# Two transformer blocks on one core: new durations in the instruction planner, and the low weight parts made on VectorE

## The chip, the cores and the metric

The kernel runs on one core of a Trainium2 chip. The metric is device time in microseconds (us) of one launch. Engine names are those of the profile: PE (TensorE matmul), PEld (its weight load), DVE (VectorE), ACT (ScalarE), POOL (GpSimd) and SP (SyncE, which here only issues DMAs).

## The reference

512 tokens of width 1024 go through two blocks, in fp32.

```python
# first block
h = rmsnorm(x); z = h @ w_in                      # 1024 x 5120
y_a = pool_mixer(z_pool) @ w_branch_a             # running means over 2, 4, 8, 16 tokens
y_b = spatial_gating(gelu(z_uv)) @ w_branch_b
x = x + (g_a * y_a + g_b * y_b) @ w_out
x = x + conv_ffn(rmsnorm(x))                      # w_up, 3-tap convolution in time, gelu(a) * b, w_down
x = x + sigmoid(rmsnorm(x) @ w_ple_gate) * (p @ w_ple)
x = rmsnorm(x)
# second block, two layers
for i in range(2):
    x = x + 0.5 * swiglu(rmsnorm(x))              # 1024 x 2816, twice, and back
    x = x + (sliding_window_attention, latent_attention)[i](rmsnorm(x))
    x = x + 0.5 * swiglu(rmsnorm(x))
```

## The kernel before

**Precision.** Each fp32 operand of a large product is split into a high part in the matmul type fp32r and a low part, the rest. `mm` (L710) then makes one product from three matmuls: high by high, high by low, low by high. So 128 rows of depth by 512 tokens are three matmuls of 128x512. For activations, `split` makes the high part on ACT and the low part on DVE. For weights, `Weights._make` (L599) loads a chunk of 128x1024 (`wr`, three buffers), casts it on ACT (`wh`, four buffers) and subtracts on POOL (`wl`, four buffers); it runs three chunks ahead of the chunk in use. Only the first chunk is subtracted on DVE, in four quarters.

**Stages, in order.** Mixer; convolutional feed-forward; the p branch; final norm and first swiglu; sliding-window attention; two swiglus; latent attention; last swiglu. A feed-forward stage (`up_down`, L908) makes 12 pairs of projections (each projection 24 matmuls of 128x512), then half of the way down, then 10 pairs, then the other half. Activations lie transposed, features on partitions and the 512 tokens in the free dimension, as eight tiles x0 to x7.

**Norms.** A stage begins with `operands` and `rstd_tok`: for each x tile a split (ACT high, DVE low, written to `op`), a square on ACT (`f`) and a DVE sum `f<-f`. Four small matmuls with the column `mcol` turn the sum into a mean for each token (`pt<-mcol,f`). PE fills the time until then with the first projections of the stage.

**The convolutional stage.** Each pair takes on DVE two reads of PSUM (`f<-ps,f`), four `SCALAR_TENSOR_TENSOR` (`f<-f,vec`), one product and one split. In the background, one chunk a pair, runs the bias of the later sliding-window attention (`plan_bias`, L1046): six DVE operations of 128x512 (`e<-poshi`, `e<-e,poslo`, `g<-e,poslo`), 24 small matmuls on PE (`pt<-rbp,g`) and two DVE additions of 128x256 (`e<-pt,con`).

**Order.** Nothing is issued where the code stands. The program is first recorded (class `Order`, L368), then `arrange` runs a list schedule: five engines with clocks of their own, a duration for each instruction (`_cost`), a latency of 150 ns from any instruction to one that depends on it (`LAT`), a transfer model, and the buffers of every pool. At each step an engine takes the ready instruction that stands first in the program and finds its buffers free. The order that results is what each engine's queue executes in sequence, on the chip with real durations: an instruction whose input is late holds up all behind it on its engine. All instructions are emitted by L586, so the profile names that line throughout; tiles tell them apart.

Of the kernel before, what the change touches and what calls it, by code (L numbers as in the profile page):

```python
# [10 lines left out]
F32 = mybir.dt.float32  # L11
# [29 lines left out]

# 1 / (2 pi) in parts of 11 bits
INV_2PI = 159154943091895335768883763372514362034459645740456448747667344
# [5 lines left out]

# ---------------------------------------------------------------- host layout  # L50

# [198 lines left out]

# ------------------------------------------------------------- issue order
#
# The program is first traced with tiles and views that stand for the real ones,
# then every engine's instructions are put in the order in which a list schedule
# over rough costs would start them, and emitted so.

# [98 lines left out]
class Instr:  # L355
    __slots__ = ("eng", "name", "args", "kw", "deps", "tiles", "cost", "new", "table", "n", "ready", "bytes", "key",
                 "rows")

# [9 lines left out]
class Order:  # L368
    LAT = 150.0
    TABLES = {AF.Gelu: "g", AF.Silu: "s", AF.Sin: "s", AF.Sigmoid: "d", AF.Exp: "e"}  # L370
# [12 lines left out]
    def _cost(self, o):  # L383
        kw, a = o.kw, o.args
        if o.name == "dma_start":
            return 60.0
        if o.eng == "tensor":
            if o.name == "transpose":
                return 107.0
            n = math.prod(kw["rhs"].shape[1:])  # L390
            dt = kw["rhs"].dtype
            if dt == F32R:
                return max(n / 2.4 + 0.5, 56.0)
            return 4 * (n / 2.4 + 2.5) if dt == F32 else max(n / 2.4 + 2.5, 27.0)
        out = kw["out"] if "out" in kw else a[0]
        src = kw.get("in_", kw.get("in0", out))
        n = max(self._size(out), self._size(src))
        psum = any(isinstance(v, View) and v.base.pool.pool_psum for v in list(kw.values()) + list(a))
        if o.eng == "scalar":
            extra = sum(isinstance(kw.get(k), View) for k in ("scale", "bias", "accum_out"))  # L400
            near = isinstance(src, View) and src.base.pool.pool_psum
            return n / 1.2 + (51 if near else 95) + 93 * extra
        if o.eng == "vector":
            if o.name == "memset":
                return 20.0
            if o.name == "reciprocal":
                return 6.3 * n + 70
            fast = o.name in ("tensor_copy", "tensor_scalar") and not psum
            extra = sum(isinstance(kw.get(k), View) for k in ("scalar", "scalar1"))
            return n / (1.92 if fast else 0.96) + 70 + 59 * extra  # L410
        if o.name == "memset":
            return 50.0
        return (3.4 if o.name == "tensor_copy" else 2.24) * n + 80

    def add(self, eng, name, args, kw):
# [28 lines left out]
        o.table = self.TABLES.get(kw.get("func")) if eng == "scalar" else None  # L444
        o.cost = self._cost(o)
        o.rows = kw["rhs"].shape[0] / P if "rhs" in kw else 1.0
        o.bytes = 0
# [5 lines left out]

    def arrange(self):
        import heapq
        count, uses = {}, {}
# [15 lines left out]
        table, dma = None, 0.0  # L472
        warm, busy, window = False, 0.0, 0.0
        done = []
# [7 lines left out]
        def fits(o):  # L482
            need = {}
            if any(id(b) not in placed and b not in o.new for b in o.tiles):
                return False
            for b in o.new:
                need[b.slot] = need.get(b.slot, 0) + 1
            for k, c in need.items():
                if free[k] < c:
                    return False  # L490
                if free[k] < c + SPARE.get(k[1], 99):
                    f, i = fifo[k], head[k]
                    while c:
                        if id(f[i]) not in placed:
                            if f[i] not in o.new:
                                return False
                            c -= 1
                        i += 1
            return True

        while len(out) < len(self.ops):
# [8 lines left out]
            for e in engines:  # L510
# [41 lines left out]
                if o.table is not None and o.table != table:  # L552
                    table = o.table
                    c += 1283.0
                clock[e] = now + c
                end = now + c
                if o.bytes:
# [4 lines left out]
                for x in after[o.n]:  # L562
                    x.ready = max(x.ready, end + (0.0 if x.eng == o.eng == "tensor" else self.LAT))
                    count[x.n] -= 1
# [7 lines left out]
            if not nxt:  # L572
                if progress:
                    continue
                stuck = [(e, self.ops[n].name, n, [b.name for b in self.ops[n].new]) for e in engines
                         for _, n in sorted(able[e])[:2]]
                raise RuntimeError(f"no order found: {stuck}")
            now = min(nxt)
        return out

# [8 lines left out]

# ---------------------------------------------------------------- on the chip  # L590

class Weights:
# [7 lines left out]
    def _make(self):  # L600
# [8 lines left out]
        for o in range(0, n, step):  # L609
            c = slice(o, o + step)  # L610
            nc.sync.dma_start(out=raw[:, c], in_=src[:, c])
            nc.scalar.copy(out=h[:, c], in_=raw[:, c])
            (nc.vector if first else nc.gpsimd).tensor_tensor(out=lo[:, c], in0=raw[:, c], in1=h[:, c].bitcast(F32),
                                                              op=ALU.subtract)
# [13 lines left out]
class Core:  # L628
# [79 lines left out]

    # products of operands in two exact parts
    def mm(self, ps, w, x, start, stop):  # L710
# [82 lines left out]

    # ------------------------------------------------------------ first block
    def mixer(self):
# [209 lines left out]

    # ----------------------------------------------------------- second block
    def final_and_ffn(self):
# [30 lines left out]

    # relative-position bias and mask of the sliding window, one table entry at
    # a time by thresholds of the distance  # L1040
    def plan_bias(self):
# [79 lines left out]
    def attn_a(self):  # L1121
# [12 lines left out]

        # heads of 64 columns brought to length one, in place
        def norms(fs, tag):
# [32 lines left out]
        norms(kf, "k")  # L1169
        # keys of the two groups side by side, zero where the groups do not meet  # L1170
        kb = [self.opp.tile([P, 2, S], F32R, name="op", tag="op") for _ in range(2)]
# [114 lines left out]

    # sine and cosine of position times frequency, by exact reduction in turns
    def plan_rope(self):
# [61 lines left out]
    def attn_b(self):  # L1350
# [6 lines left out]
        nc.vector.tensor_copy(out=idb, in_=self.c("id", P))  # L1357
        # latents and the shared key part, tokens on partitions, two token tiles at a time
        wl = []
# [48 lines left out]

        # one over the length of four heads of 96 columns in four token tiles
        def lengths(ss, tag):  # L1410
# [77 lines left out]

        # keys of tile st against queries st..3, three banks
        dst = [(0, 0), (1, 0), (2, 0), (1, 3 * P)]  # L1490
# [153 lines left out]
```

## Time and profile before

| | |
|---|---|
| three timed runs | 2784.25, 2785.83, 2788.27 us |
| span of the profiled execution, first to last instruction | 2782.1 us |
| PE busy in it | 2679.4 us (96%) |
| DVE, ACT, POOL busy | 1376.1 (49%), 954.7 (34%), 1225.4 us (44%) |
| subtraction of the low weight parts on POOL | 1107.6 us in 467 instructions |
| granted TensorE clock, mean | 0.983 |

The page gives no time for the profiled execution but its span. The median of the runs is 3.7 us above it: what lies before the first and behind the last instruction. PE's busy time is a union of modelled spans: in a stretch in which PE never waits it reads 100%.

### The profile page before, as it was taken

How to read it: one execution, taken by the hardware profiler on the slowest of the kernel's cores; microseconds unless marked ns; L12 is line 12 of the kernel's file. 1: busy time of each engine (PE TensorE's matmuls, PEld its weight loads, DVE VectorE, ACT ScalarE, POOL GpSimd, SP SyncE). 2: the span in 40 equal slices, each digit the busy share in tenths (PEclk: the TensorE clock that was granted, in tenths of full speed). 3: DMA queues.
4: the chain of work that ended last, by engine and by line, in shares of the span. 5: the costliest groups of instructions: out<-in, count | busy, mean ns of one | idle time of the engine just before them, and what ended most of it. 6: DMA issues, size and time to landing. Idle time of an engine off the chain costs nothing. (4 is left out here: it accounts for less than half of the span.)

```text
span 2782.1 us, 32524 instructions
## 1 busy us (share of the span) xinstructions
PE 2679.4 (96%) x12768; PEld 2187.3 (79%) x12768; DVE 1376.1 (49%) x2193; ACT 954.7 (34%) x1486; POOL 1225.4 (44%) x664
## 2 busy tenths in 40 slices
PE   7999998999799899999999999999999899999999
PEld 5788886888677788889778888888888766688887
DVE  5506369949937861335743313343133676533141
ACT  3324333323334222334633223323223475432221
POOL 4543443353334344444534444444444443344443
PEclk9999999999899999999999999999999999999999
DMA  4232223333323333333222233322333201233322
GB/s 148 95 99 89 93 92 102 93 114 106 91 70 97 99 99 98 99 99 105 78 84 93 97 99 99 97 86 97 98 99 96 58 12 31 72 99 99 98 92 83
DMA packets 102617, 254.31 MB, mean 91 GB/s; under 512 B 37360, under 2 KB 39024, under 8 KB 102464
## 3 DMA queue, kind: packets, MB, share of 16 engines
q1 hardware_dynamic: 101840, 250.26, 28.4%
q8 instruction: 101, 1.65, 0.2%
q0 software_dynamic: 624, 1.97, 0.2%
q14 instruction: 52, 0.43, 0.1%
HBM read 242.76 MB, written 9.44 MB: 91 GB/s over the span
## 5 line engine op out<-in xcount | busy, mean ns | idle before, releaser
L586 PE MATMUL ps<-op,wh 128*128 128x512 f32 x6624 | 2069.9, 393 | 35.9 <-ACT op L586 24.4
L586 POOL TENSOR_TENSOR wl<-wr,wh 128x1024 fp32r<-128x1024 f32 (+3 forms) x467 | 1107.6, 2374 | 1393.3 <-ACT wh L586 1380.0
L586 PEld LDWEIGHTS ps<-op,wh 128*128 128x128 f32 x6624 | 1250.5, 189 | 304.7 <-ACT op L586 27.0
L586 PE MATMUL ps<-op,wl 128*128 128x512 f32 x3312 | 1299.7, 392 | 0.0
L586 ACT CAST wh<-wr 128x1024 fp32r<-128x1024 f32 (+3 forms) x471 | 468.1, 994 | 1236.7 <-PE ps L586 760.4
L586 PEld LDWEIGHTS ps<-op,wl 128*128 128x128 f32 x3312 | 627.4, 189 | 132.2 <-issue 1.0
L586 DVE TENSOR_TENSOR f<-ps,f 128x512 f32<-128x512 f32 x260 | 178.8, 688 | 532.9 <-PE ps L586 510.9
L586 DVE TENSOR_TENSOR op<-f,op 128x512 fp32r<-128x512 f32 x136 | 226.2, 1665 | 68.8 <-ACT op L586 68.0
L586 DVE TENSOR_TENSOR f<-f 128x512 f32<-128x512 f32 x213 | 203.1, 954 | 46.0 <-POOL f L586 19.8
L586 DVE SCALAR_TENSOR_TENSOR x<-ps,x 128x512 f32<-128x512 f32 x64 | 44.2, 691 | 339.0 <-PE ps L586 339.0
L586 ACT CAST op<-f 128x512 fp32r<-128x512 f32 x136 | 84.2, 621 | 211.1 <-DVE f L586 211.1
L586 PE MATMUL ps<-wh,op 128*128 128x256 f32 (+3 forms) x608 | 149.9, 333 | 4.8 <-ACT f L586 2.5
L586 PEld LDWEIGHTS ps<-wh,op 128*128 128x128 f32 x608 | 106.0, 194 | 15.6 <-ACT f L586 3.1
L586 ACT ACTIVATE f<-f 128x512 f32<-128x512 f32 x142 | 89.0, 627 | 77.8 <-DVE f L586 77.1
L586 DVE SCALAR_TENSOR_TENSOR f<-f,vec 128x512 f32<-128x512 f32 x88 | 104.5, 1188 | 8.9 <-ACT f L586 8.6
L586 DVE SCALAR_TENSOR_TENSOR op<-x,vec,op 128x512 fp32r<-128x512 f32 x64 | 84.4, 1324 | 48.1 <-ACT op L586 48.1
L586 PE MATMUL ps<-wl,op 128*128 128x256 f32 (+3 forms) x304 | 100.4, 330 | 0.0
L586 DVE TENSOR_TENSOR x<-ps,x 128x512 f32<-128x512 f32 x56 | 38.4, 688 | 98.6 <-PE ps L586 98.6
L586 ACT ACTIVATE op<-x,vec 128x512 fp32r<-128x512 f32 x64 | 45.8, 721 | 73.1 <-DVE x L586 72.8
L586 PE MATMUL pt<-con,opf 128*128 128x128 f32 (+1 forms) x348 | 54.5, 280 | 8.2 <-DVE opf L586 3.5
L586 PEld LDWEIGHTS ps<-wl,op 128*128 128x128 f32 x304 | 59.0, 194 | 3.5 <-issue 0.3
L586 DVE TENSOR_TENSOR g<-e,poslo 128x512 bf16<-128x512 f32 x56 | 61.4, 1098 | 0.1
(181 smaller groups left out, 1366.1 us busy)
## 6 DMA issues: line engine op xcount, KB each, us to landing
wr<-in_w SPq DMA_DIRECT2D x411, 512.0 KB, 3.3
wr<-in_w SPq DMA_DIRECT2D x40, 256.0 KB, 2.7
bias<-e SPq DMA_DIRECT2D x28, 256.0 KB, 2.7
opf<-bias SPq DMA_DIRECT2D x16, 448.0 KB, 6.0
x<-in_xT SPq DMA_DIRECT2D x8, 256.0 KB, 6.7
out_y<-x SPq DMA_DIRECT2D x8, 256.0 KB, 2.0
wr<-in_w SPq DMA_DIRECT2D x4, 416.0 KB, 3.1
wr<-in_w SPq DMA_DIRECT2D x12, 128.0 KB, 2.1
```

Source lines behind the costliest of these rows:

```text
L586: getattr(getattr(self.nc, o.eng), o.name)(*[real(a) for a in o.args], **{k: real(v) for k, v in o.kw.items()})
```

## The change

Five things. (1) `Weights._make` subtracts on DVE for every chunk, no longer on POOL. (2) The durations in `_cost` are other numbers: a 128x512 matmul in fp32r costs the planner 227.0 ns instead of 213.8, an fp32 matmul and a bf16 one a little less, POOL's operations 2.0 or 2.35 ns an element instead of 3.4 or 2.24. (3) The latency is a number for each engine. (4) The planner has a `port`: POOL's compute instructions, and those DVE instructions that `_port` names, start one after another in its model. (5) `arrange` tries again with more spare buffers where a plan sticks, in place of an error.

```diff
-    LAT = 150.0
+    LAT = {"tensor": 203.0, "vector": 111.0, "scalar": 128.0, "gpsimd": 90.0, "sync": 34.0}
...
             if dt == F32R:
-                return max(n / 2.4 + 0.5, 56.0)
+                return max(n / 2.4 + 13.7, 56.0)
...
+    def _port(self, o):
+        if o.eng == "gpsimd":
+            return o.name != "dma_start"
+        if o.eng != "vector" or o.name == "memset":
+            return False
+        vs = [v for v in list(o.kw.values()) + list(o.args) if isinstance(v, View) and self._size(v) > 1]
+        near = [v for v in vs if not v.base.pool.pool_psum]
+        if o.name in ("tensor_copy", "tensor_scalar"):
+            return len(near) == len(vs)
+        return o.name in ("tensor_tensor", "scalar_tensor_tensor", "tensor_tensor_reduce") and len(near) > 2
...
-                clock[e] = now + c
-                end = now + c
+                begin = now
+                if o.port:
+                    begin = max(now, port)
+                    port = begin + c
+                clock[e] = begin + c
+                end = begin + c
...
             nc.scalar.copy(out=h[:, c], in_=raw[:, c])
-            (nc.vector if first else nc.gpsimd).tensor_tensor(out=lo[:, c], in0=raw[:, c], in1=h[:, c].bitcast(F32),
+            nc.vector.tensor_tensor(out=lo[:, c], in0=raw[:, c], in1=h[:, c].bitcast(F32),
                                                               op=ALU.subtract)
```

What the new plan does to the queues is seen at three places. The first is DVE at the end of the latent attention, where each of the last projections is added to an x tile (`x4<-ps`), split (`op<-x4,vec`), and its square added to the sum (`f<-f`). Before, from x4 to x6:

```order
L586 TENSOR_TENSOR x4_125<-ps_18271,x4_125 128x512
L586 SCALAR_TENSOR_TENSOR op_18308<-x4_125,vec_84,op_18308 128x512
L586 TENSOR_TENSOR f_18212<-f_18212,f_18313 128x512
L586 TENSOR_TENSOR x5_127<-ps_18298,x5_127 128x512
L586 SCALAR_TENSOR_TENSOR op_18335<-x5_127,vec_84,op_18335 128x512
L586 TENSOR_TENSOR x6_129<-ps_18321,x6_129 128x512
```

And in the changed kernel, over the same tiles:

```order
L617 TENSOR_TENSOR x4_121<-ps_18272,x4_121 128x512
L617 TENSOR_TENSOR wl_18304<-wr_18233,wh_18296 128x1024
L617 SCALAR_TENSOR_TENSOR op_18307<-x4_121,vec_84,op_18307 128x512
L617 TENSOR_TENSOR f_18211<-f_18211,f_18311 128x512
L617 TENSOR_TENSOR x5_123<-ps_18298,x5_123 128x512
L617 TENSOR_TENSOR wl_18331<-wr_18259,wh_18321 128x1024
L617 SCALAR_TENSOR_TENSOR op_18334<-x5_123,vec_84,op_18334 128x512
L617 TENSOR_TENSOR x6_125<-ps_18324,x6_125 128x512
```

One weight subtraction now stands between each addition to an x tile and its split; the rest keeps its order. The second place is DVE in the second half of the convolutional stage, with the bias in the background. Before, somewhat under one pair:

```order
L586 TENSOR_TENSOR f_4734<-ps_4936,f_2873 128x512
L586 TENSOR_TENSOR e_4981<-e_4981,poslo_2999 128x512
L586 TENSOR_TENSOR e_5004<-poshi_2979 128x512
L586 SCALAR_TENSOR_TENSOR f_5000<-f_4734,vec_84,f_5000 128x512
L586 TENSOR_TENSOR g_4974<-e_4981,poslo_2999 128x512
L586 SCALAR_TENSOR_TENSOR f_5000<-f_4734,vec_84,f_5000 128x512
```

In the changed kernel, from a read of PSUM on:

```order
L617 TENSOR_TENSOR f_4776<-ps_4861,f_2868 128x512
L617 TENSOR_TENSOR e_4831<-pt_4906,con_129 128x8x32
L617 TENSOR_TENSOR e_4839<-pt_4906,con_129 128x8x32
L617 TENSOR_TENSOR wl_4944<-wr_4763,wh_4903 128x1024
L617 SCALAR_TENSOR_TENSOR f_4937<-f_4776,vec_84,f_4937 128x512
L617 TENSOR_TENSOR e_4958<-poshi_2975 128x512
L617 SCALAR_TENSOR_TENSOR f_4937<-f_4776,vec_84,f_4937 128x512
```

A subtraction stands between each read of PSUM and the first operation on it, two for a pair, and all of the bias work is still there. The third place is PE at the very start, around the four matmuls that make the first mean (`pt<-mcol`). Before, in the middle of the second projection:

```order
L586 MATMUL ps_224<-op_168,wl_222 128x512
L586 MATMUL ps_224<-op_172,wh_212 128x512
L586 MATMUL pt_253<-mcol_86,f_143 128x1 x4
L586 MATMUL ps_224<-op_172,wh_212 128x512
L586 MATMUL ps_224<-op_172,wl_222 128x512
```

In the changed kernel, in the middle of the third:

```order
L617 MATMUL ps_225<-op_162,wh_217 128x512 x2
L617 MATMUL ps_225<-op_162,wl_234 128x512
L617 MATMUL pt_284<-mcol_86,f_137 128x1 x4
L617 MATMUL ps_225<-op_166,wh_217 128x512 x2
L617 MATMUL ps_225<-op_166,wl_234 128x512
```

The mean is asked for 21 matmuls later. In the later norms PE's order is the same to within a few matmuls.

## Rows read from the trace of the kernel before

**Rows 1.** Cores: span and mean granted TensorE clock.
```profile
core 0: 2782.1 us, clock 0.983
```
**Rows 2.** PE's waits, whole span: total us, times, longest.
```profile
PE pt L586 <- DVE f L586: 30.4, 10, 6.7
PE ps L586 <- ACT op L586: 24.8, 6, 14.6
PE pt L586 <- DVE g L586: 11.8, 6, 4.5
```
**Rows 3.** Stretches: length, busy us (x instructions) per engine, granted clock, DMA share, GB/s.
```profile
430.00:475.00 45.00, 33.99 (x214) 26.70 (x214) 43.52 (x57) 13.08 (x17) 18.88 (x7) 0.96 0.29 87
...
741.00:766.00 25.00, 8.21 (x23) 5.53 (x22) 21.52 (x27) 8.59 (x12) 7.48 (x3) 0.59 0.26 83
...
1459.00:1816.00 357.00, 357.00 (x1575) 295.28 (x1574) 117.70 (x118) 106.11 (x128) 165.90 (x66) 1.00 0.30 96
...
2180.00:2243.00 63.00, 51.69 (x254) 42.58 (x253) 50.53 (x176) 35.27 (x81) 25.77 (x45) 0.92 0.16 45
...
2411.00:2425.00 14.00, 7.55 (x26) 6.06 (x25) 9.15 (x21) 2.72 (x4) 4.82 (x3) 0.63 0.26 77
```
**Rows 4.** Groups by form, whole span, DVE and POOL: busy us, mean ns, idle before.
```profile
L586 DVE TENSOR_TENSOR op<-f,op 128x512 fp32r<-128x512 f32 x136 | 226.2, 1665 | 68.8 <-ACT op L586 68.0
L586 DVE TENSOR_TENSOR f<-f 128x512 f32<-128x512 f32 x213 | 203.1, 954 | 46.0 <-POOL f L586 19.8 <-ACT f L586 16.1
L586 DVE TENSOR_TENSOR f<-ps,f 128x512 f32<-128x512 f32 x260 | 178.8, 688 | 532.9 <-PE ps L586 510.9 <-ACT f L586 21.8
...
L586 DVE TENSOR_TENSOR rst<-rtok 128x4 f32<-128x4 f32 x30 | 4.9, 163 | 1.0
...
L586 POOL TENSOR_TENSOR wl<-wr,wh 128x1024 fp32r<-128x1024 f32 x411 | 1032.5, 2514 | 1279.6 <-ACT wh L586 1266.2 <-PE ps L586 13.2
```
**Rows 5.** Timeline of DVE, end of the latent attention: start, length.
```profile
2402.04 1.60 DVE L586 SCALAR_TENSOR_TENSOR op<-x,vec,op 128x512 fp32r<-128x512 f32 x1 [0.79 <-ACT op L586]
2403.56 2.91 DVE L586 TENSOR_TENSOR f<-f 128x512 f32<-128x512 f32 x1
...
2410.01 2.60 DVE L586 SCALAR_TENSOR_TENSOR op<-x,vec,op 128x512 fp32r<-128x512 f32 x1 [0.20 <-ACT op L586]
2412.54 2.82 DVE L586 TENSOR_TENSOR f<-f 128x512 f32<-128x512 f32 x1
```
**Rows 6.** Timeline of POOL, the same stretch.
```profile
2403.54 2.38 POOL L586 TENSOR_TENSOR wl<-wr,wh 128x1024 fp32r<-128x1024 f32 x1 [0.45 <-ACT wh L586]
2409.38 5.44 POOL L586 TENSOR_TENSOR wl<-wr,wh 128x1024 fp32r<-128x1024 f32 x2 [3.45 <-ACT wh L586]
```
**Rows 7.** Groups by form from 631 to 760 us, DVE and POOL.
```profile
L586 DVE SCALAR_TENSOR_TENSOR f<-f,vec 128x512 f32<-128x512 f32 x38 | 46.5, 1223 | 2.8 <-ACT f L586 2.6
L586 DVE TENSOR_TENSOR e<-e,poslo 128x512 f32<-128x512 f32 x20 | 21.6, 1082 | 0.0
L586 DVE TENSOR_TENSOR g<-e,poslo 128x512 bf16<-128x512 f32 x20 | 21.3, 1066 | 0.0
...
L586 POOL TENSOR_TENSOR wl<-wr,wh 128x1024 fp32r<-128x1024 f32 x20 | 49.8, 2497 | 79.5 <-ACT wh L586 75.3 <-PE ps L586 4.2
```
**Rows 8.** Timeline of DVE from 740 us, operations without a wait.
```profile
740.83 0.74 DVE L586 SCALAR_TENSOR_TENSOR f<-f,vec 128x512 f32<-128x512 f32 x1
...
742.21 0.68 DVE L586 TENSOR_TENSOR g<-e,poslo 128x512 bf16<-128x512 f32 x1
742.81 0.68 DVE L586 TENSOR_TENSOR e<-poshi 128x512 f32<-128x512 f32 x1
```
**Rows 9.** Groups by form, DVE, first 14 us.
```profile
L586 DVE TENSOR_TENSOR wl<-wr,wh 128x256 fp32r<-128x256 f32 x4 | 1.7, 425 | 3.0 <-ACT wh L586 3.0
```
**Rows 10.** Groups by form, DVE, from 2183 to 2220 us.
```profile
L586 DVE SCALAR_TENSOR_TENSOR bly<-rst,bly 128x4 f32<-128x4 f32 x6 | 3.1, 521 | 0.1
...
L586 DVE TENSOR_TENSOR rst<-bly 128x4 f32<-128x4 f32 x6 | 2.6, 435 | 0.1
```

More of the change, by code (lines that the diff above doesn't have):

```diff
@@ L356 @@
     __slots__ = ("eng", "name", "args", "kw", "deps", "tiles", "cost", "new", "table", "n", "ready", "bytes", "key",
-                 "rows")
+                 "rows", "port")
 class Engine:
@@ L392, in _cost @@
             if dt == F32R:
-                return max(n / 2.4 + 0.5, 56.0)
-            return 4 * (n / 2.4 + 2.5) if dt == F32 else max(n / 2.4 + 2.5, 27.0)
+                return max(n / 2.4 + 13.7, 56.0)
+            return 4 * (n / 2.4 + 1.0) if dt == F32 else max(n / 2.4 + 2.0, 28.0)
         out = kw["out"] if "out" in kw else a[0]
@@ L412, in _cost @@
             return 50.0
-        return (3.4 if o.name == "tensor_copy" else 2.24) * n + 80
+        return (2.0 if o.name == "tensor_copy" else 2.35) * n + 60
+    def _port(self, o):
[8 more added lines that the diff above has]
+        return o.name in ("tensor_tensor", "scalar_tensor_tensor", "tensor_tensor_reduce") and len(near) > 2
     def add(self, eng, name, args, kw):
@@ L445, in add @@
         o.cost = self._cost(o)
+        o.port = self._port(o)
         o.rows = kw["rhs"].shape[0] / P if "rhs" in kw else 1.0
@@ L454, in arrange, with _arrange @@
     def arrange(self):
+        spare = dict(SPARE)
+        for _ in range(40):
+            left = {id(b): b.left for o in self.ops for b in o.tiles}
+            out, stuck = self._arrange(spare)
+            if not stuck:
+                return out
+            for o in self.ops:
+                for b in o.tiles:
+                    b.left = left[id(b)]
+            for tag in stuck:
+                if tag in spare:
+                    spare[tag] += 1
+        raise RuntimeError(f"no order found: {stuck}")
+    def _arrange(self, spare):
         import heapq
@@ L472, in arrange @@
         table, dma = None, 0.0
-        warm, busy, window = False, 0.0, 0.0
+        warm, busy, window, port = False, 0.0, 0.0, 0.0
         done = []
@@ L490, in fits @@
                     return False
-                if free[k] < c + SPARE.get(k[1], 99):
+                if free[k] < c + spare.get(k[1], 99):
                     f, i = fifo[k], head[k]
@@ L562, in arrange @@
                 for x in after[o.n]:
-                    x.ready = max(x.ready, end + (0.0 if x.eng == o.eng == "tensor" else self.LAT))
+                    x.ready = max(x.ready, end + (0.0 if x.eng == o.eng == "tensor" else self.LAT[o.eng]))
                     count[x.n] -= 1
@@ L574, in arrange @@
                     continue
-                stuck = [(e, self.ops[n].name, n, [b.name for b in self.ops[n].new]) for e in engines
-                         for _, n in sorted(able[e])[:2]]
-                raise RuntimeError(f"no order found: {stuck}")
+                return out, sorted({b.slot[1] for e in engines for _, n in sorted(able[e])[:2] for b in self.ops[n].new})
             now = min(nxt)
-        return out
+        self.end, self.spare = now, spare
+        return out, []
     def emit(self):
```

## The prediction

> **What bounds the kernel now.** I read the table of stretches first, then PE's waits, then DVE and POOL by form, and last the timeline at the longest waits. Where PE has nothing to wait for, it is full: 1459 to 1816 us shows 357.00 us busy of 357.00 at a granted clock of 1.00, 1575 matmuls, so one each 0.227 us [rows 3]. Most of the kernel is like that, and there DVE is busy for a third of the time. The change takes nothing off PE, so all it can win lies in the stretches where PE waits, and in the clock behind such waits. The waits have three main owners: 30.4 us in ten places for a sum on DVE (`pt<-f`, the mean of each norm), 24.8 us for `op` (split activations), and 11.8 us for `g` (the bias) [rows 2]. I see an eleventh place in the table, the first tiles of the latent attention, with 63.00 - 51.69 = 11.3 us without PE [rows 3]. After a wait the clock is lower: 0.63 in 2411 to 2425, 0.59 in 741 to 766 [rows 3]. Over the span the mean is 0.983 [rows 1], so 2 x 0.017 x 2782 = 95 us ran at 1.2 GHz in place of 2.4; a good part of that is the waits themselves.
>
> Why is DVE late in those places? Not for want of time: by the forms, an operation that reads PSUM takes 688 ns whatever else goes on, while the same size with both inputs in SBUF takes 954 or 1665 ns in the mean [rows 4], though 0.68 us is what it takes undisturbed [rows 8]. The timeline shows when it is longer. At 2403.56 a sum takes 2.91 us: POOL's subtraction runs from 2403.54 to 2405.92, and the sum ends 0.55 us after it. At 2410.01 and 2412.54 it is the same, 2.60 and 2.82 us under POOL's pair of 5.44 us [rows 5, 6]. So a DVE operation with two SBUF inputs waits for the POOL operation that is under way and then does its own work. That wait is booked as busy time.
>
> **What the change costs and removes.** The 467 subtractions go from POOL, where one of 128x1024 takes 2.51 us [rows 4], to DVE. No row shows that size on DVE. The 128x256 form takes 0.425 us [rows 9], a 128x512 one 0.68 [rows 8]; the difference is 1.0 ns an element, so 1024 should take 0.68 + 0.51 = 1.19 us. Neighbours without a wait start 0.60 us apart though they last 0.68 [rows 8], so in a full queue I charge 1.11. An upper bound is POOL's own 2.51 us, a lower one the elements alone, 1.02; I take 1.11, close to the row of the same operation.
>
> *Norms (30.4 us).* At the end of the latent attention the four long operations of the timeline hold 0.86 + 2.23 + 1.86 + 2.14 = 7.1 us of waiting for POOL [rows 5]. Four subtractions of 1.11 come in, 4.4 us. If they merely filled DVE, 2.7 us of the 6.45 (14.00 - 7.55 [rows 3]) would be won. But the new order puts each between the addition to x and the split, where DVE now idles 0.79 us for ACT [rows 5]. From the fourth-last tile on, DVE then has 4 x (0.60 + 1.11 + 0.67 + 0.60) = 11.9 us, while PE has three more groups of 12 matmuls and 19 of the next stage before it asks for the mean: 55 x 0.227 = 12.5 us. The sum is ready by then, and what is late next is only the semaphore. At the start of the kernel PE asks for the mean 21 matmuls later, 4.8 us, by order alone. I leave 0.6 us in each of the ten places and win 24 of 30.4 us; the bounds are 13 (the share 2.7 of 6.45) and 27.
>
> *Second half of the convolution (741 to 766, 16.8 us without PE).* Between 631 and 760 DVE has no idle time worth the name. Its excess is 38 x (1.223 - 0.74) = 18.4, 20 x (1.082 - 0.68) = 8.0 and 20 x (1.066 - 0.68) = 7.7, together 34.1 us [rows 7, 8]. In come 20 subtractions, 22.2 us. DVE ends 12 us sooner; I take 11 of the 16.8, with bounds of 0 and 16.8.
>
> *Other waits for `op`* (24.8 less the 16.1 of that place): 5 of 8.7 us, bounds 3 and 8. *The bias at 430 to 475*, 11.0 us without PE, nearly all of the 11.8 us for `g` [rows 2, 3]: DVE is busy 43.52 of 45, so the same trade holds at a third of the length; 6 us, bounds 0 and 11.8. *First tiles of the latent attention:* operations on four columns take 435 and 521 ns in the mean [rows 10] where the same in the norms takes 163 [rows 4], and they form one chain: 6 x 0.27 + 6 x 0.36 = 3.8 us of waiting for POOL in these two forms alone. But POOL keeps its own products there, and subtractions now stand in the same chain: 4 us, bounds 0 and 8.
>
> *Clock.* In 2411 to 2425, (1 - 0.63) x 14 x 2 = 10.4 us at the lower level [rows 3], of which some 6 are busy, so 3 us lost. Where the wait goes I let the dip go: 12 us over all places, bounds 5 and 25.
>
> *What is added.* DVE executes in sequence. A subtraction waits for the cast on ACT, and that for PE to free a buffer; behind it in the queue stand PSUM reads, on which PE waits when its five banks are full. On POOL such a wait held up nobody: 1266 us of idle before the subtraction came from the cast [rows 4]. In the full stretches this is covered, since DVE needs 118 us of 357 and the 66 subtractions that POOL did there [rows 3] add 73. At the eleven places it isn't, and I charge each with one subtraction, 12 us in all; bounds 0 and 30. POOL's other work, about a tenth of its time, goes on holding DVE where it stands; the change doesn't touch it. The other durations in the planner move the order in the attentions, which I can't price and count at nothing; bounds -5 and +5.
>
> Sum: 24 + 11 + 5 + 6 + 4 + 12 = 62, less 12, is 50 us. From the span, 2782.1 - 50 = 2732; with the 3.7 us by which the median of the runs lies above the span, 2736 us.
>
> **A rule against it.** Rows 8 show DVE operations that start 0.60 us apart and last 0.68: each starts before the one ahead has ended. The Trainium skill, "VectorE: DVE Perf Modes", section "The DRAIN you can't avoid", says that the pipeline empties after every VectorE operation before the next starts (with the exception of one that isn't held). By that rule the subtraction would cost its whole 1.19 us and every other operation its whole length. The trace doesn't agree for these neighbours.
>
> **The rivals.** *DVE becomes the bound of the convolution.* A pair with its bias chunk, by the order, is 10 operations of 128x512 with two tensors, four `SCALAR_TENSOR_TENSOR`, two of 128x256 and two subtractions: by pitch 10 x 0.60 + 4 x 0.67 + 2 x 0.34 + 2 x 1.11 = 11.6 us, against 48 x 0.227 = 10.9 on PE and the small bias matmuls. With whole lengths, or bubbles of 0.1 us an operation, it is 6.8 + 3.0 + 0.8 + 2.4 = 13.0, and before the ten pairs took 129 us, 12.9 each. Then the 17 us of those two places and 2 of clock aren't won: 2736 + 19 = 2755. For it speaks how close 11.6 is to PE's time; against it, the pitch. *More is won:* no new waits and the whole upper bound of the norms, the convolution and half of the dips: 2736 - 12 - 3 - 6 - 5 = 2710. *The long operations are not POOL's doing,* so the change doesn't do what its planner models: DVE keeps its lengths and gets 20 subtractions in 631 to 760 and about 30 in the first half, 50 x 1.19 = 60 us on a queue that is full: 2845. The forms that read PSUM and don't stretch speak against it [rows 4].
>
> *Slower: the subtraction at the head of DVE's queue.* Place: the 22 pairs of the convolution, 42 subtractions behind a PSUM read each. POOL waited for the cast 75.3 us over 20 subtractions, 3.8 each [rows 7]. If the plan places them 1.6 us too early in the mean, PE, which has no slack there, pays 42 x 1.6 = 67 us, against 50 won: 2803. It decides from 50 / 42 = 1.2 us of waiting each. Against it: DVE is behind PE there, so that the cast should be long done when its turn comes.
>
> **Chances.** Forecast (2715 to 2750) 0.62, more won 0.10, convolution bound by DVE 0.15, slower by waits in the queue 0.07, no effect on the long operations 0.02; 0.04 for the space between, where new waits eat the gain. What a measurement of this kernel can tell from no change is about 0.2%, 5.6 us. So faster 0.87, same 0.04, slower 0.09. The range takes in the rival at 2755 and its neighbourhood, and reaches 2706 to 2778; the forecast's own is 2715 to 2750.
>
> **What would show it.** In the changed profile the mean of `op<-f,op` falls from 1665 to about 700 ns and `f<-f` from 954 to about 700; DVE shows 411 subtractions near 1.19 us; PE's wait for `pt<-f` falls from 30.4 to some 6 us and 741 to 766 loses most of its hole; the mean clock rises towards 0.99. The rival of the convolution would show as waits for `op` or `g` of the old size with DVE full; the queue rival as DVE idle before `wl` for `wh`. The prediction is wrong if the sums are short but PE's waits stay, since then DVE's lateness wasn't what PE waited for.

## The result, and the profile after

The changed kernel takes 2696.73 us in the median (2695.72 to 2698.03, four runs), beside 2787.05 us for the kernel before (2784.25 to 2788.57, four runs): ratio 0.9678, interval 0.9664 to 0.9692. It is faster by 3.2%, 90 us, where 50 us were forecast, and lies 9 us under the lower end of the range: right in the direction, wrong in the size.

The span of the profiled execution, on which all rows below rest, falls by 86.5 us. The 90 us are of medians: a run is 1.8 us longer than its span (2697.42 against 2695.6 here), not 3.7 as the text on the time before reads it, so the execution profiled before was some 3 us faster than its median, and the one after 0.7 us slower.

The page of the changed kernel: span, then busy time, share of the span and instructions of the engines.

```profile
span 2695.6 us, 32222 instructions
...
PE 2650.3 (98%) x12768; PEld 2163.3 (80%) x12768; DVE 1533.8 (57%) x2660; ACT 957.7 (36%) x1486; POOL 125.8 (5%) x197
```

PE executes the same 12768 instructions as before, yet it is busy 29.1 us less (2679.4 before); its idle time, span less busy, fell from 102.7 to 45.3 us, by 57.4. So 57.4 us are waits that went, and 29.1 us are the same matmuls at a higher clock. The mean granted clock, for which [rows 1] had 0.983:

```profile
core 0: 2695.6 us, clock 0.997
```

What the lower level does to PE's busy time is seen around the longest wait of before, in the stretch from 741 to 766 us with its clock of 0.59: ahead of the wait neighbours start 0.23 us apart (744.49, 744.72), behind it 0.43 (760.94, 761.37), at the lower of the two levels, 1.2 in place of 2.4 GHz.

```profile
744.49 0.39 PE L586 MATMUL ps<-op,wl 128*128 128x512 f32 x1
744.72 0.57 PE L586 MATMUL ps<-op,wh 128*128 128x512 f32 x1
759.92 1.22 PE L586 MATMUL ps<-op,wh 128*128 128x512 f32 x2 [14.63 <-ACT op L586]
760.94 0.63 PE L586 MATMUL ps<-op,wl 128*128 128x512 f32 x1
761.37 1.05 PE L586 MATMUL ps<-op,wh 128*128 128x512 f32 x2
```

PE's waits, whole span (total, times, longest); the last three rows answer to [rows 2]:

```profile
PE ps L617 <- ACT wh L617: 8.2, 3, 7.5
PE pt L617 <- POOL opf L617: 6.7, 7, 1.6
PE pt L617 <- DVE op L617: 5.7, 2, 4.7
PE ps L617 <- ACT op L617: 4.4, 2, 3.0
...
PE pt L617 <- DVE g L617: 1.1, 1, 1.1
PE pt L617 <- DVE f L617: 0.7, 2, 0.6
```

Ten waits for the norms' sums, 30.4 us, are 0.7 us; `op` fell from 24.8 to 4.4, `g` from 11.8 to 1.1. The longest wait left is for the first weights at the start. Two waits grew by some us, both in the attentions; before, they were:

```profile
PE pt L586 <- POOL opf L586: 1.0, 1, 1.0
PE pt L586 <- DVE op L586: 0.6, 2, 0.3
```

DVE by form, as in [rows 4] (busy us, mean ns, idle before):

```profile
L617 DVE TENSOR_TENSOR wl<-wr,wh 128x1024 fp32r<-128x1024 f32 x411 | 506.4, 1232 | 297.2 <-ACT wh L617 296.0
L617 DVE TENSOR_TENSOR f<-ps,f 128x512 f32<-128x512 f32 x260 | 179.1, 690 | 428.1 <-PE ps L617 422.7 <-ACT f L617 5.2
L617 DVE TENSOR_TENSOR f<-f 128x512 f32<-128x512 f32 x213 | 145.9, 685 | 7.7 <-POOL f L617 5.0 <-ACT f L617 2.0
L617 DVE TENSOR_TENSOR op<-f,op 128x512 fp32r<-128x512 f32 x136 | 93.7, 691 | 65.0 <-ACT op L617 64.9
```

A subtraction takes 1.23 us, half of what it took POOL. `op<-f,op` went from 1665 to 691 ns and `f<-f` from 954 to 685; the form that reads PSUM is what it was. And DVE idles 296 us before `wl` for the cast on ACT, which POOL used to do. The stretches that answer to [rows 3], and the end of the latent attention:

```profile
385.00:765.00 380.00, 379.86 (x2097) 309.87 (x2097) 313.86 (x519) 138.75 (x174) 1.07 (x2) 1.00 0.34 104
...
1412.00:1760.00 348.00, 347.91 (x1537) 287.39 (x1536) 157.72 (x195) 101.41 (x123) 0.00 (x0) 1.00 0.29 96
...
2324.00:2338.00 14.00, 13.98 (x66) 11.39 (x65) 12.35 (x26) 8.25 (x11) 0.00 (x0) 1.00 0.48 151
```

The first is the whole convolutional stage, with both places of before in it: PE is busy 379.86 of 380 us. The third was 7.55 of 14 us at a clock of 0.63. DVE there, in place of [rows 5]:

```profile
2325.57 0.69 DVE L617 TENSOR_TENSOR x<-ps,x 128x512 f32<-128x512 f32 x1
2326.17 1.22 DVE L617 TENSOR_TENSOR wl<-wr,wh 128x1024 fp32r<-128x1024 f32 x1
2327.30 0.75 DVE L617 SCALAR_TENSOR_TENSOR op<-x,vec,op 128x512 fp32r<-128x512 f32 x1
2327.97 0.69 DVE L617 TENSOR_TENSOR x<-ps,x 128x512 f32<-128x512 f32 x1
...
2333.96 0.69 DVE L617 TENSOR_TENSOR f<-f 128x512 f32<-128x512 f32 x1
```

PE waits for nothing here, and a subtraction takes 1.13 us of the queue (2326.17 to 2327.30). The last sum ends at 2334.65, and PE's next row starts at 2334.70, with no idle time before it:

```profile
2334.70 1.05 PE L617 MATMUL pt<-mcol,f 128*128 128x1 f32 x8
```

Length and PE's idle time by stage, in us (idle is the length less PE busy, from the table of stretches; a stage ends with the last update of x7):

| stage | length before | after | idle before | after |
|---|---|---|---|---|
| mixer | 398.6 | 383.9 | 22.2 | 11.2 |
| convolution | 416.9 | 380.5 | 29.9 | 0.1 |
| p branch to first swiglu | 446.5 | 429.6 | 12.2 | 3.5 |
| sliding attention | 187.4 | 183.3 | 9.1 | 11.2 |
| two swiglus | 728.0 | 722.2 | 5.3 | 0.1 |
| latent attention | 237.9 | 231.5 | 17.2 | 15.4 |
| last swiglu | 366.8 | 364.6 | 6.7 | 3.9 |

The gain comes mostly from the mixer, the convolution and the stage behind it. In the attentions PE's idle time stays what it was. They are 4.1 and 6.4 us shorter, but about 5 of these 10 us are no gain: PE executes 11 and 13 fewer matmuls before their ends and about as many more in the next stage (an estimate, at 0.227 us each).

### The profile page after: what moved, and what is told of

Read it like the earlier page. It is cut to its first block, busy times and chain, and to the rows that moved or that the text cites. A ratio compares the mean times of both kernels' runs of the same rounds, so it can differ in the third digit from the quotient of the medians.

```text
span 2695.6 us, 32222 instructions
## 1 busy us (share of the span) xinstructions
PE 2650.3 (98%) x12768; PEld 2163.3 (80%) x12768; DVE 1533.8 (57%) x2660; ACT 957.7 (36%) x1486; POOL 125.8 (5%) x197
## 5 line engine op out<-in xcount | busy, mean ns | idle before, releaser
L617 DVE TENSOR_TENSOR wl<-wr,wh 128x1024 fp32r<-128x1024 f32 (+3 forms) x471 | 546.8, 1161 | 314.3 <-ACT wh L617 312.9
L617 DVE TENSOR_TENSOR f<-f 128x512 f32<-128x512 f32 x213 | 145.9, 685 | 7.7 <-POOL f L617 5.0
L617 DVE TENSOR_TENSOR op<-f,op 128x512 fp32r<-128x512 f32 x136 | 93.7, 691 | 65.0 <-ACT op L617 64.9
L617 DVE SCALAR_TENSOR_TENSOR f<-f,vec 128x512 f32<-128x512 f32 x88 | 65.6, 745 | 2.5 <-ACT f L617 2.3
L617 PEld LDWEIGHTS pt<-con,opf 128*128 128x128 f32 (+1 forms) x348 | 40.7, 140 | 32.0 <-issue 10.6
L617 DVE SCALAR_TENSOR_TENSOR op<-x,vec,op 128x512 fp32r<-128x512 f32 x64 | 48.7, 765 | 25.0 <-ACT op L617 25.0
```

Source lines behind the costliest of these rows:

```text
L617: getattr(getattr(self.nc, o.eng), o.name)(*[real(a) for a in o.args], **{k: real(v) for k, v in o.kw.items()})
```

## The experiments

Two theories stood after the first comparison. L: POOL's subtraction held DVE, DVE was late for PE, and the subtraction's move alone brings the gain. P: the planner's measured durations bring it.

**The subtraction alone, with the old planner.**

```diff
-            (nc.vector if first else nc.gpsimd).tensor_tensor(out=lo[:, c], in0=raw[:, c], in1=h[:, c].bitcast(F32),
+            nc.vector.tensor_tensor(out=lo[:, c], in0=raw[:, c], in1=h[:, c].bitcast(F32),
```

> The kernel before with one edit: the low weight parts on DVE; the planner keeps its old durations, its 150 ns and has no port. Theory L (what was won is the end of DVE's waiting for POOL, and the clock that follows from it): 2700 to 2725 us, `op<-f,op` near 690 ns, PE's waits for sums and for `op` mostly gone. Theory P (the measured durations put the queues in an order in which nobody waits): 2745 to 2775 us, with short DVE operations but PE's waits at the norms and behind the convolution kept at half of their size or more.

Measured: 2692.44 us, ratio 0.9668 (0.9654 to 0.9683). This one line brings the whole gain and more than L expected. The old planner arranges the program anew with it, so PE's order differs somewhat too (the table further down counts it); the runs with POOL's repeats and with late sums, which keep an order as it is, show the hold and the waits by themselves.

**The new planner alone, subtraction on POOL:** the same line the other way, in the changed kernel.

> The changed kernel with one edit undone: the low weight parts stay on POOL (all but the first chunk), planned with the new durations, latencies and the port. Theory L: 2765 to 2790 us, `op<-f,op` and `f<-f` as long as before (over 1500 and 900 ns). Theory P: 2720 to 2745 us, since the planner now knows that the two engines exclude each other and puts the operations apart.

Measured: 2720.9 us, ratio 0.9772 (0.9758 to 0.9787): P's number. The plan alone brings 64 us. Two of DVE's forms, and PE's wait for the sums:

```profile
L617 DVE TENSOR_TENSOR op<-f,op 128x512 fp32r<-128x512 f32 x136 | 241.9, 1779 | 73.2 <-ACT op L617 72.7
L617 DVE TENSOR_TENSOR f<-f 128x512 f32<-128x512 f32 x213 | 204.5, 962 | 30.8 <-POOL f L617 11.1 <-ACT f L617 9.7
```
```profile
PE pt L617 <- DVE f L617: 10.2, 3, 6.3
```

These forms are as slow as before, so on the whole it is not that the planner puts the operations apart, as P had it; but PE waits for the sums a third as long. So 92 us from the one edit, 64 from the other, and 90 from both: they are two cures for one ill, and don't add.

**The changed kernel without the port.**

```diff
-        o.port = self._port(o)
+        o.port = False
```

> The changed kernel, its planner without the port (no instruction counts as one that excludes another). POOL has 126 us of work left. Both theories: 2690 to 2710 us; what differs lies in the two attentions. Over 2715 would say that the port's model in the plan carries a part of the gain.

Measured: 2694.12 us, ratio 0.9676 (0.9661 to 0.969), as the changed kernel's 0.9678. With POOL nearly empty (125.0 us busy) the port gains nothing.

**POOL busy again, plan untouched.** Every subtraction of a chunk is repeated on POOL as it is emitted, into a tile that nobody reads.

```diff
+            if isinstance(out, View) and out.base.name == "wl" and o.eng == "vector" and math.prod(out.shape[1:]) > 256:
+                t = self.echo.real()[:, :math.prod(out.shape[1:])]
+                self.nc.gpsimd.tensor_tensor(out=t, in0=kw["in0"], in1=kw["in1"], op=ALU.subtract)
```

> The changed kernel with its plan untouched; behind every subtraction on DVE, POOL makes the same one again into a tile that nobody reads (the output is not affected). DVE's queue is that of the changed kernel, the subtractions on it included. Theory L: 2760 us or more, `op<-f,op` back over 1500 ns, PE's waits back at the norms and in the convolution, the clock below 0.985. Theory P: 2697 to 2715 us, since the order is the same. If the long DVE operations were not POOL's doing, nothing changes at all.

Measured: 2897.52 us, ratio 1.0408 (1.0387 to 1.0428), 201 us over the changed kernel. DVE by form, and the repeats on POOL:

```profile
L618 DVE TENSOR_TENSOR wl<-wr,wh 128x1024 fp32r<-128x1024 f32 x411 | 737.2, 1794 | 228.6 <-ACT wh L618 228.1
L618 DVE TENSOR_TENSOR f<-f 128x512 f32<-128x512 f32 x213 | 369.0, 1733 | 10.2 <-POOL f L618 9.0 <-ACT f L618 0.5
L618 DVE TENSOR_TENSOR f<-ps,f 128x512 f32<-128x512 f32 x260 | 178.0, 686 | 99.3 <-PE ps L618 93.9 <-ACT f L618 5.2
L618 DVE TENSOR_TENSOR op<-f,op 128x512 fp32r<-128x512 f32 x136 | 98.9, 729 | 63.7 <-ACT op L618 63.7
```
```profile
L622 POOL TENSOR_TENSOR echo<-wr,wh 128x1024 f32<-128x1024 f32 x411 | 1267.4, 3084 | 1155.0 <-ACT wh L618 1129.1 <-issue 17.3 <-DVE f L618 5.0
```

This shows the hold: the same instructions in the same order take 1733 instead of 685 ns, while the form with an input in PSUM keeps its 686 ns. Sorted by whether a repeat on POOL runs meanwhile, the 221 operations `f<-f` fall apart cleanly: 98 without one take 0.68 us, 94 under one and just behind a subtraction 2.83 us, the other 29 under one 1.43 us. `f<-ps,f` takes 0.68 to 0.69 us in either case (131 with, 129 without). So it matters what stands beside POOL's operation: `op<-f,op`, the longest of before, is only 729 ns here, against the expectation, as 119 of its 136 meet none. POOL pays too, 3084 instead of 2514 ns. The Trainium skill, "SBUF — State Buffer", section "SBUF: two separate sides", states it so: a VectorE operation with two SBUF inputs and a GpSimd operation that reads SBUF exclude each other, and whichever comes second is blocked for the whole of the other. These rows agree. The repeats also keep `wr` and `wh` longer; their part in the 201 us wasn't separated.

**What the plan's 64 us consist of.** Two runs with the subtraction on POOL: the new durations and latencies without the port (the plan-only kernel with `o.port = False`), and the port with the old numbers:

```diff
-    LAT = {"tensor": 203.0, "vector": 111.0, "scalar": 128.0, "gpsimd": 90.0, "sync": 34.0}
+    LAT = {"tensor": 150.0, "vector": 150.0, "scalar": 150.0, "gpsimd": 150.0, "sync": 150.0}
...
-                return max(n / 2.4 + 13.7, 56.0)
+                return max(n / 2.4 + 0.5, 56.0)
```

> The kernel before with the new durations and latencies in the planner, without the port, the subtraction on POOL. The plan alone, port included, ran 2720.9 us, 64 us under before, though DVE's operations stayed long. Theory K (the plan gains because its port puts PE's requests where a DVE held by POOL can meet them): without the port little is left, 2760 to 2790 us, PE's wait for the sums back over 20 us. Theory N (the plan gains by its better durations): 2710 to 2735 us, that wait near 10 us.

> The kernel before with the port in the planner and nothing else: old durations, latency 150 ns throughout, the subtraction on POOL. Theory K: the port carries the plan's gain, 2710 to 2740 us, PE's wait for the sums about 10 us. Theory N: without the new durations the port does little, 2765 to 2790 us.

Measured: the numbers alone 2794.16 us, ratio 1.0034 (1.0021 to 1.0047), slower than before; the port alone 2747.01 us, 0.9866 (0.9851 to 0.9881). Both lie on K's side, each some us above what K gave; with the port alone PE still waits 16.6 us for the sums, not about 10. The measured durations bring nothing by themselves, the port 39 us, and the two together 64. How the port helps can be counted: the weight matmuls that PE has executed when it asks for the mean, at the ten norms.

| kernel | matmuls ahead of each mean, against the kernel before |
|---|---|
| numbers alone | 0, -1, -1, -2, -10, -3, -1, -1, -1, -3 |
| port alone | +45, +7, +13, +50, +23, +15, +37, +7, +6, +25 |
| both (plan alone) | +43, +6, +9, +13, +23, +10, +20, +6, +4, +18 |
| subtraction alone | +10, +2, +2, +2, +16, +4, +12, +2, 0, +9 |
| changed kernel | +21, 0, 0, 0, +11, -1, +4, 0, -1, +2 |

A planner that knows of the hold lets PE do other work until the late sum is there (152 matmuls of 0.227 us are 34.5 us, against 30.4 us of waits). More ahead isn't always better: the port alone has 228, and gains less. Nor are the norms the whole of the plan's gain: of the 43.5 us of idle time that went (102.7 to 59.2), the sums are 20.2; in the convolution PE's waits of 16.1 us for `op` and 11.5 for `g` went to none and 3.5, with 3.5 for `f` new, and which move of the order did that was not traced. The changed kernel asks as early as the one before at most norms (21 matmuls later at the first, and 11 at the fifth, where the text on the change has "a few"), and doesn't wait because the sum is early. The plan of before was one for a DVE that nobody holds.

**What the clock costs.** The changed kernel in its own order, each sum over x delayed by seven additions on DVE.

```diff
         for o in self.arrange():
+            for _ in range(7 if o.n in self.late else 0):
+                t = self.echo.real()
+                self.nc.vector.tensor_tensor(out=t[:, S:], in0=t[:, :S], in1=t[:, :S], op=ALU.add)
```

> The changed kernel in its own order; in front of the last addition of each of the eight token sums of squares over x (bound for pt<-mcol) DVE executes seven additions of 128x512 into a tile that nobody reads, 7 x 0.60 = 4.2 us. The sums of the changed kernel end just when PE asks for them, so each should cost PE a wait of about 4 us, 34 us for eight. Theory C (a wait of PE costs the clock behind it again: between the two kernels 29 us of PE's busy time went with 57 us of idle, 0.5 for one): PE's busy time rises by some 17 us from 2650, the total is 2740 to 2755. Theory D (the clock's share came from something else than such waits): PE's busy time stays within 5 us of 2650, the total is 2728 to 2736.

Measured: 2773.45 us, ratio 0.9961 (0.9946 to 0.9976). There are ten such sums, not eight as I wrote, and each costs 4.9 us, not 4.2. The page's span and PE, PE's wait for the sums, and the last norm:

```profile
span 2774.7 us, 32291 instructions
...
PE 2681.7 (97%) x12768; PEld 2189.7 (79%) x12768; DVE 1582.1 (57%) x2731; ACT 957.6 (35%) x1486; POOL 125.7 (5%) x197
```
```profile
PE pt L621 <- DVE f L621: 49.2, 10, 5.1
```
```profile
2404.00:2420.00 16.00, 11.03 (x44) 8.78 (x42) 11.40 (x28) 2.01 (x3) 0.00 (x0) 0.79 0.24 76
```

Idle time rose by 47.7 us (from 45.3 to 93.0), PE's busy time by 31.4: 0.66 us of clock for one of waiting. Theory C holds, and the total is above its 2755 because the waits are 49 us instead of 34, and the clock's share 0.66 instead of 0.5; D leaves no room for 31.4 us of PE's own. The price is not a constant: the second dose of subtractions below gives 0.45 (32.9 of busy time for 73.9 of idle), the subtraction alone against before 0.41 (26.4 for 65.1), and POOL's repeats 0.35 (52.1 for 150.8).

**Is POOL's rest worth emptying?** All products, squares and copies of the two attentions moved from POOL to DVE, planned anew; for instance:

```diff
-                    nc.gpsimd.tensor_tensor(out=e[n], in0=e[n], in1=den[:, n:n + 1].to_broadcast([P, (n + 1) * P]),
-                                            op=ALU.mult)
+                    nc.vector.tensor_scalar(out=e[n], in0=e[n], scalar1=den[:, n:n + 1], scalar2=None, op0=ALU.mult)
```

> The changed kernel with the products, squares and copies that POOL still computes in the two attentions moved to DVE, the divisions by the denominators as tensor_scalar; the planner arranges it anew. Theory L (what POOL still computes goes on holding DVE): PE loses some 19 us in the two attentions now (33.0 - 23.65 around 1262 to 1295, 40 - 30.29 around 2110 to 2150), about half of it goes and some clock with it, 2680 to 2692 us. Theory Q (these chains are as long on DVE as on POOL and DVE becomes late with other things): 2695 to 2710 us.

Measured: 2700.99 us, ratio 0.9699 (0.9684 to 0.9713). L was wrong here. The start of the latent attention has less idle time than in the changed kernel (5.32 of 40 us, against 9.71), but a lower clock (0.83, against 0.91). First this kernel, then the changed one:

```profile
2110.00:2150.00 40.00, 34.68 (x151) 26.17 (x150) 29.93 (x135) 23.77 (x54) 0.00 (x0) 0.83 0.19 57
```
```profile
2110.00:2150.00 40.00, 30.29 (x151) 24.76 (x150) 31.07 (x120) 23.94 (x53) 7.88 (x24) 0.91 0.19 57
```

Both rows have 151 matmuls in 40 us. Less idle time does not mean less waiting here: at the lower clock the same matmuls fill more of it. In the last 10 us PE is busy throughout, with fewer matmuls (this kernel first, then the changed one):

```profile
2140.00:2150.00 10.00, 10.00 (x40) 7.55 (x39) 4.48 (x13) 4.13 (x9) 0.00 (x0) 0.62 0.09 26
```
```profile
2140.00:2150.00 10.00, 8.48 (x44) 6.60 (x43) 6.32 (x19) 4.32 (x8) 0.00 (x0) 0.86 0.16 48
```

Over the span PE idles 5.3 us less and is busy 9.3 us more, and by the last updates of x7 the latent attention lasts 236.8 us against 231.5. Why the clock fell lower there stays open.

**A second dose of subtractions,** each executed twice on DVE, in the changed kernel's order.

```diff
-                self.nc.gpsimd.tensor_tensor(out=t, in0=kw["in0"], in1=kw["in1"], op=ALU.subtract)
+                self.nc.vector.tensor_tensor(out=t, in0=kw["in0"], in1=kw["in1"], op=ALU.subtract)
```

(The line removed is that of the run with POOL's repeats.)

> The changed kernel in its own order, with every subtraction of a whole chunk executed twice in a row on DVE, the second time into a tile that nobody reads: 1.14 us more for each of 411. It asks how much room the first dose left. Theory E (the first dose cost nothing because it just filled idle time; the plan is at the edge): in the convolution DVE is busy 294 of 355 us and gets some 62 x 1.14 = 71 us more, 10 over the time there; at the ten norms four or five subtractions make each sum some 5 us later, 50 us, and the clock takes 0.6 of it: 60 + 36, about 2790 us, 2770 to 2815. Theory R (room is left, since DVE is busy 57% over the span): under 2730 us.

Measured: 2804.53 us, ratio 1.0068 (1.005 to 1.0086), 108 us over the changed kernel, and slower than before the change. PE's waits, and the convolution:

```profile
PE pt L618 <- DVE g L618: 30.0, 24, 9.9
PE pt L618 <- DVE f L618: 23.1, 10, 5.3
PE ps L618 <- ACT op L618: 15.1, 5, 6.6
```
```profile
395.00:800.00 405.00, 367.16 (x1993) 295.40 (x1992) 372.11 (x567) 131.94 (x162) 1.07 (x2) 0.97 0.31 93
```

The total is E's: though DVE is busy only 57% of the span, the first dose had nearly filled what was free at the norms and in the convolution. The split is not E's: it gave 50 us to the norms and 10 to the convolution, and the sums cost 23.1 us of waiting, while PE is idle for 37.8 us in the convolution (405 less 367.16), most of it for `g`.

**Subtraction alone against the whole change,** on one chip, four runs each.

> The changed kernel unaltered, as the measure for the run beside it: 2694 to 2699 us.

> The kernel before with the subtraction on DVE and nothing else, beside the changed kernel on the same chip. If the new plan adds nothing once DVE is not held: within 3 us of the changed kernel. If it costs by asking for the sums at the last moment (they end 0.05 us ahead of the request, 0.2 to 0.7 us with the old plan): 3 to 6 us under it.

Measured: 2698.28 us (2696.42 to 2699.53), and 2692.61 us (2692.24 to 2692.86) for the subtraction alone, 5.7 us under it. That is the fastest kernel here: one line, and the old planner. The reason that I gave is not the cause, since the changed kernel waits 0.7 us for its sums. The difference lies in the attentions: there the subtraction alone leaves PE idle 7.9 and 10.5 us, the whole change 11.2 and 15.2. First the subtraction alone, then the whole change:

```profile
1198.00:1380.00 182.00, 174.15 (x1148) 151.36 (x1147) 120.07 (x358) 95.10 (x251) 40.98 (x42) 0.97 0.27 93
2101.00:2331.00 230.00, 219.52 (x1078) 154.32 (x1077) 165.38 (x452) 133.15 (x321) 59.74 (x128) 0.99 0.14 42
```
```profile
1194.00:1377.30 183.30, 172.15 (x1152) 150.63 (x1151) 119.03 (x358) 95.67 (x250) 40.74 (x42) 0.97 0.27 90
2099.50:2331.00 231.50, 216.35 (x1063) 150.99 (x1063) 166.37 (x448) 134.16 (x320) 62.32 (x128) 0.99 0.13 39
```

By the last updates of x7 the two attentions last 181.5 and 226.2 us with the subtraction alone, 183.3 and 231.5 with the whole change, and 182.0 and 228.8 in the run without the port. So the port, which keeps DVE's and POOL's operations apart in the plan, accounts for 4 of these 7 us; which of the other numbers costs the rest wasn't tried. In the mixer the whole change is the shorter one, by 2.8 us.

## Why the prediction was right in direction and wrong in size

The mechanism held: the sums are short, the waits behind them went, the stretches that were full stayed full. The sum by its terms, in us of the span:

| term | forecast (bounds) | measured |
|---|---|---|
| norms | 24 (13 to 27) | 29.7 (30.4 to 0.7) |
| second half of the convolution | 11 (0 to 16.8) | 16.8 |
| bias, 430 to 475 | 6 (0 to 11.8) | 11.0 |
| other waits for `op` | 5 (3 to 8) | 4.3 (8.7 to 4.4) |
| first tiles of the latent attention | 4 (0 to 8) | 0.9 |
| other places, in sum | 0 (-5 to 5) | -5.3 |
| clock | 12 (5 to 25) | 29.1 |
| new waits in DVE's queue | -12 (-30 to 0) | none at the norms and in the convolution; the rest is in the line of other places |
| sum | 50 | 86.5 |

**The clock, 17 us short,** is the step that failed most. I read 3 us of loss behind one wait of 6.45 us, 0.47 for one, and then took 12 us for 50 us of waits, 0.24 for one. The change itself measured 29.1 for 57.4, 0.51, and the late sums, which put nothing but waits back, 0.66. The row was right; I didn't carry it to the other places.

**The charge for new waits, 12 us, met nothing at the norms and in the convolution,** where 0.7 and 0.1 us of waiting are left. It was counted twice. The chain of 11.9 us at the norms already held four subtractions of 1.11 us, and the convolution's balance 20 of them; I then charged one more for each of eleven places, for a danger that I had argued away in the rival. DVE does wait for the cast, 296 us of idle before `wl`, but where PE leaves it time: in the convolution it is busy 313.86 of 380 us and PE loses nothing. That it isn't free for ever the second dose shows.

**The order in the attentions, counted at nothing,** is where waits did come: PE's waits for `opf` on POOL rose from 1.0 to 6.7 us and those for `op` on DVE from 0.6 to 5.7. They are in the -5.3 of the other places, just under its bound. The subtraction alone, planned with the old numbers, waits 4.9 us for `opf` on POOL and not at all for `op` on DVE there, and is 5.7 us faster in all.

**Norms, convolution and bias, 16 us short.** At the norms the working gave the upper bound and I took less: 11.9 us of DVE under 12.5 of PE says that the whole wait goes. In the convolution the working itself gave only 12 of the 16.8 us. From the first PSUM read of the last ten pairs to their last split DVE takes 121.1 us (592.3 to 713.4), where it took 138.2 (623.6 to 761.8). One form over these two stretches, before and after:

```profile
L586 DVE SCALAR_TENSOR_TENSOR f<-f,vec 128x512 f32<-128x512 f32 x40 | 49.5, 1238 | 3.7 <-ACT f L586 3.6
L617 DVE SCALAR_TENSOR_TENSOR f<-f,vec 128x512 f32<-128x512 f32 x40 | 29.8, 746 | 0.0
```

The excess went as worked out; but the 3.7 us of idle time before this form went too, and four of the 60 bias operations, 2.4 us, now stand behind the last pair. The working had neither. The bias at 430 to 475 us was scaled from it. The pitch was right (1.11 forecast, 1.13 in the queue; 1.19 forecast and 1.23 measured for its length). So the rival "more is won" (2710) came nearest, and it lacked the clock.

**Latent attention.** The chain that I blamed did get short, and the hole stayed. `bly` and `rst<-bly` after, 521 and 435 ns in [rows 10], then the stretch (63 us, of which 51.69 were busy):

```profile
L617 DVE TENSOR_TENSOR rst<-bly 128x4 f32<-128x4 f32 x6 | 1.0, 173 | 0.1
L617 DVE SCALAR_TENSOR_TENSOR bly<-rst,bly 128x4 f32<-128x4 f32 x6 | 1.0, 162 | 0.2
```
```profile
2102.00:2165.00 63.00, 52.57 (x271) 42.07 (x269) 48.10 (x180) 35.87 (x83) 17.41 (x43) 0.95 0.14 41
```

The two stretches don't hold the same work, 271 matmuls against 254, so the idle time alone can't price the chain. But PE's waits there have no single owner any more: from 2099 to 2160 us `opf` on POOL 3.0 us, `opf` on DVE 2.1, and three on ACT of 1.4 to 1.9. The chain stood beside the wait; that it alone was what PE waited for is not what the rows show.

**The rivals.** DVE did not become the bound of the convolution, and neighbours go on starting 0.60 us apart, a subtraction 1.13; the rule of the Trainium skill, "VectorE: DVE Perf Modes", section "The DRAIN you can't avoid", as the prediction weighed it, would have the next operation wait the whole 0.69 and 1.22, and these rows don't. The second dose is what that rival would have looked like. The slower rival, a subtraction at the head of the queue, shows as idle time that costs PE nothing. The third, that long operations aren't POOL's doing, is refuted by POOL's repeats. What I had no case for is that the planner alone could do two thirds of it: I counted its other numbers at nothing, and with POOL still subtracting they are worth 64 us.

## What to carry to other kernels

An engine that runs a written order loses where chip and plan differ: one can make the chip like the plan (take away what holds DVE) or the plan like the chip (model the hold), and here either gave most of it, so the gains of the two are not added. Where a chain is worked out against the time that covers it, and the cover is longer, take the whole wait, and count each added instruction once. A wait of PE's costs more than its length: with the clock behind it, 1.35 to 1.66 times in five of these pairs of runs; the run with POOL's rest emptied went the other way, with less idle time and more busy time.

## What was not expected of the hardware

The price of the hold, as the move of this one operation from POOL to DVE shows it, is 92 us of 2785, though DVE has the subtractions to do as well. It works both ways: beside the repeats DVE's `f<-f` went from 0.68 to 2.83 us, and POOL's subtraction from 2514 to 3084 ns. And idle time is no measure of waiting where the clock differs: the same 151 matmuls in 40 us left 5.32 us idle at a clock of 0.83, and 9.71 at 0.91.
